# A hybrid decoder layer: plain products for the second pair of column tiles, one weight split fewer in every pair, and a reordered startup

## The chip, the cores and the metric

The kernel runs on one core of one Trainium2 chip. The metric is device time in microseconds (us), lower is better. Below, PE is the matrix engine (TensorE), DVE the vector engine, ACT the scalar engine, POOL is GpSimd and SP the engine that issues most transfers; PEld is the weight load of PE. A few tenths of a per cent separate repeated runs.

## What is computed

One layer is applied to a prompt of 1024 tokens and to 64 sample tokens (8 requests of 8 tokens). In short:

```
h      = RMSNorm(x, norm_pre)
proj   = h @ w_in                       # 1024 x 6656: seven slices of 512, three gates of 1024
a      = pool_mix(p_in) * silu(p_gate)
u      = c_val * sigmoid(c_glu)         # c_val: columns 1024.., c_glu: columns 1536..
bconv  = silu(LayerNorm(dwconv31(u))) * silu(c_gate)
cattn  = softmax(q @ mk) @ mv * silu(x_gate)      # mk, mv = RMSNorm(mem) @ w_mem_kv
merged = sum_n sigmoid(gate_n) * (branch_n @ w_branch[n])
y      = x + RMSNorm(merged @ w_out, norm_post)
```

The outputs are y for the prompt and the samples, the new memory keys and values, and the new states of the pooling and the convolution.

## The kernel before

**Numbers.** All is float32 in memory. For a product each operand is split by `hilo` (L74) into two float16 parts: ACT writes the high part (L75), DVE or POOL the rest (L77 without a factor, L79 with one). `mm3` (L81) then issues three matmuls for each block of 128 rows of the contraction (L85, L88, L89). An operand of 512 x 128 weights so costs one ACT and one DVE instruction for its split, and twelve matmuls for each 512 tokens.

**Pairs.** `w_in` is worked through in pairs of column tiles, 256 columns at a time, 26 pairs in all. The first pair (the first half of c_glu, columns from FIRST) is done with plain products inside `startup`. Each of the other 25 is a call of `pair` (L446), the first of them for c_val. With two tiles r, two halves kh of the contraction and two halves of the tokens a plain pair has eight products of 12 matmuls. `pair` uses seven: sums of the four weight blocks a11, a12, a21, a22 meet sums of the four input blocks. The input blocks and their sums are split once, into the seven sections B11, B21, B22, T1, T2, T3, T4 of the tile BO; the first half of the tokens as columns of h gives B11 and B21, the second gives B22 and (in two tiles b12) the block that `startup` alone uses; T1 to T4 are differences of both halves.

A pair is seven stages. `base0` (L494) splits a21 and a22, negates the second row of raw weights on ACT (L498) and adds them with an accumulating transfer issued by POOL (L499), which gives s1 = -(a21 + a22). `base1` (L502) splits a11 and a12 and issues three more accumulating transfers (L505 to L507) for s3, s2 and s4. The preps split the sums. `m0` to `m6` are the products and `e0` to `e6` take the results out of the matrix engine's memory: L513 is a copy on ACT, L466 (`post`) a scaled addition on DVE. `m5` also does the sample tokens with a11, a12, a22 and a21 against BS, the split sample columns.

**Order.** The stage list is emitted by the loop at the end of `hybrid_layer_kernel` (LDPR = 12 stages ahead for the loads, 3 for the preps, BASE = 8 for the sums). After each stage some steps of the convolution (`conv_step`) and of the side jobs (`job_step`: `states`, `mem_kv`, attention heads, ...) follow, at the two rates that RATES gives for each section. All this is the order in which the program is written; a scheduler then places the instructions on the engines' queues, and each queue runs in its order. Buffers are few: 20 of tag Q, 13 split weight blocks (ws), 4 raw weight pairs (raw), 4 + 4 banks (pm, pb).

**Startup.** `startup` (L236) is a generator, run at the end of the function with pieces of the first call of `pair` between its yields. It loads eight tiles of x (xt[0] to xt[7]), takes their squares on ACT (`rstds`, L169), turns them by `flip` (L225; four transposes on PE for 128 columns), multiplies by the norm's factors (L264) and splits the first half of the tokens into B11 and B21. Between these splits the squares of xt[4] to xt[7] are taken; then come those of the sample tile xs and of the two memory tiles. The first product `first(0, 0)` follows, then the scaling of xt[4:6] on ACT and xt[6:8] on DVE (L221, L223), the second halves by `second_half(k)` for k = 0 to 3 (L290: two flips, L292 and L295 on DVE, and splits into b12, B22 and T1), the splits of T2, and T3 and T4 from subtractions on POOL (L312, L313). The program puts products between: `first(1, 0)`, and a11 x B11 and a12 x B21 of the c_val pair.

Of the kernel before, what the change touches and what calls it, by code (L numbers as in the profile page):

```python
# [38 lines left out]
RATES = [(1.1, 2.2), (1.2, 1.4), (0.9, 1), (1, 1.2), (1.3, 1.4), (0.6, 1.8), (0.8, 0.9), (1.3, 0.2), (0.8, 1)]  # L39
# [7 lines left out]
def hybrid_layer_kernel(ctx, tc, i, o):  # L47
# [121 lines left out]
    def rstds(xs):  # L169
        ss = tiny([P, len(xs)])[: xs[0].shape[0]]  # L170
        for t, x in enumerate(xs):
            nc.scalar.activation(junk[: x.shape[0]], x, AF.Square, accum_out=ss[:, t : t + 1])
        return rstd_of(ss, 1.0 / D)

    BO = cst.tile([P, 7, 2, 4, HALF], F16, name="BO")
    junk = BO[:, 6].rearrange("p a k n -> p (a k n)")[:, : 2 * D].bitcast(F32)
# [24 lines left out]
    xt += [load(i["x_prompt"][0, t * P : (t + 1) * P, :], P) for t in range(8, 8)]  # L201
    xs = load(i["x_sample"].rearrange("b s d -> (b s) d"), NS)
    mems = [load(i["mem_prompt"][0, t * P : (t + 1) * P, :], P) for t in range(2)]
# [11 lines left out]
    BS = cst.tile([P, 2, KT, NS], F16, name="BS")  # L215
    g_pre = cst.tile([P, KT], F32, name="g_pre")
# [14 lines left out]
    def bo(n, k):  # L231
        return BO[:, n, 0, k, :], BO[:, n, 1, k, :]
# [3 lines left out]
    def startup():  # L236
# [24 lines left out]
        for k in range(KT):  # L261
# [20 lines left out]
        first(0, 0, [lambda k: bo(B11, k), lambda k: bo(B21, k)])  # L282
        scale_x(xt[4:6], rs_[0], True)
        scale_x(xt[6:8], rs_[1], False)
        first_w(1)
        first_w(3)
        b12 = [Q([P, 2, 2, HALF], F16) for _ in range(2)]
        tq = [Q([P, 2, HALF]) for _ in range(4)]

        def second_half(k):  # L290
# [6 lines left out]
            hilo(tq[k][:, 0], *bo(T1, k), -1.0)  # L297

        second_half(0)
        yield  # L300
        first(1, 0, [lambda k: bo(B11, k), lambda k: bo(B21, k)])
        yield
        for k in range(1, 4):
            second_half(k)
            yield
        for k in range(4):
            hilo(tq[k][:, 1], *bo(T2, k), -1.0)
        for r in range(2):
            first(r, HALF, [lambda k: (b12[k // 2][:, 0, k % 2], b12[k // 2][:, 1, k % 2]), lambda k: bo(B22, k)])
            for k in (2 * r, 2 * r + 1):  # L310
                t3, t4 = half(), half()
                nc.gpsimd.tensor_tensor(t3, tq[k][:, 1], hx[k][:, 0], ALU.subtract)  # L312
                nc.gpsimd.tensor_tensor(t4, hx[k][:, 1], tq[k][:, 1], ALU.subtract)  # L313
                hilo(t3, *bo(T3, k))
                hilo(t4, *bo(T4, k), eng=nc.gpsimd)
            if r:
                break
            nc.vector.tensor_scalar(xs, xs, xs_r, None, ALU.mult)
# [7 lines left out]
            hilo(hs_, BS[:, 0].rearrange("p k n -> p (k n)"), BS[:, 1].rearrange("p k n -> p (k n)"))  # L326
# [9 lines left out]
    def mem_kv():  # L336
        memT = [Q([P, 2, KT // 2, NMEM], F16) for _ in range(2)]
# [103 lines left out]
    def mm_smp(out, w, kh, start, stop):  # L441
        mm3(out, [(w[:, 0, k, :], w[:, 1, k, :], BS[:, 0, 4 * kh + k, :], BS[:, 1, 4 * kh + k, :]) for k in range(4)], start, stop)

    early = {}

    def pair(c0, dest, block, smp, sc=1.0 / WS):  # L446


        v = {}
# [21 lines left out]
        def prep0():  # L471
            if not ahead:
                prep_a11()
# [11 lines left out]
        def prep5():  # L485
            spl("a22", lambda: A(1, 1))
            spl("a21", lambda: A(1, 0))
# [6 lines left out]
        def base0():  # L494
            spl("a21", lambda: A(1, 0))
# [54 lines left out]
        def m5():  # L550
            v["s"] = pm()
            mm_smp(v["s"][:, :NS], v["w", "a11"], 0, True, False)
            mm_smp(v["s"][:, :NS], v["w", "a12"], 1, False, True)
# [779 lines left out]
    for _ in start:  # L1333
        pass
# [68 lines left out]
```

## Time and profile before

| what | value |
|---|---|
| runs of the kernel before | 931.22, 933.86, 935.12 us, median 933.86 us |
| the profiled execution | 930.47 us, of it the span of the profile 928.5 us |
| PE busy | 856.7 us (92%), 5765 matmuls |
| DVE busy | 732.8 us (79%), 1141 instructions |
| ACT busy | 453.3 us (49%), 964 instructions |
| POOL busy | 362.7 us (39%), 384 instructions |
| mean granted PE clock | 0.972 |

Times in the views are us from the start of the span. A busy PE is not a PE at its peak: the span of a matmul overlaps that of the next, so that the distance of two starts is what one costs. The profile attributes an instruction to the line of a helper (L75, L79), and the tile names tell which call it is: ws are split weights, BO the split inputs, raw the loaded weights.

### The profile page before, as it was taken

To read this page: it belongs to the slowest core of one execution; us is meant where nothing else is said; L and a number is where in the kernel's file an instruction comes from. 1 tells how busy PE (TensorE), PEld (TensorE's weight loads), DVE (VectorE), ACT (ScalarE), POOL (GpSimd) and SP (SyncE) were. 2 spreads that over 40 slices of the span, in tenths; PEclk is the share of its full clock that TensorE was granted. 3 is DMA by queue.
4 is the path that set the end of the run, shared out by engine and by line. 5 is a ranking of instruction groups with operands and counts; after the bars stand their busy time and mean duration, and the time that the engine had idled before them with its cause. 6 is when DMAs were issued, how large, how long until landed. Compare 5 with 4: busy or idle time off the path is not lost. (4 is left out here: it accounts for less than half of the span.)

```text
span 928.5 us, 15208 instructions
## 1 busy us (share of the span) xinstructions
PE 856.7 (92%) x5765; PEld 459.7 (50%) x5765; DVE 732.8 (79%) x1141; ACT 453.3 (49%) x964; POOL 362.7 (39%) x384
## 2 busy tenths in 40 slices
PE   5869999899999879999988989999999999977996
PEld 4325445454555445455444445555555555544542
DVE  4798598999967699999998977548565544699886
ACT  8757536654653614323345444446344443545542
POOL 1463243344243260311244665526364212276500
PEclk8889999999999889999999999999999999989998
DMA  8625742224466223244443335545554657311232
GB/s 300 175 47 161 202 107 55 59 70 114 117 223 159 92 38 91 59 91 93 101 106 86 79 92 100 120 115 106 117 114 114 127 131 226 95 35 46 70 125 91
DMA packets 99237, 103.23 MB, mean 111 GB/s; under 512 B 5230, under 2 KB 71780, under 8 KB 99148
## 3 DMA queue, kind: packets, MB, share of 16 engines
q1 hardware_dynamic: 82748, 68.24, 23.4%
q0 software_dynamic: 16416, 34.02, 20.4%
q8 instruction: 45, 0.74, 0.3%
q14 instruction: 28, 0.23, 0.1%
HBM read 62.37 MB, written 6.33 MB: 74 GB/s over the span
## 5 line engine op out<-in xcount | busy, mean ns | idle before, releaser
L85 PE MATMUL pm<-BO,ws 128*128 128x512 f16 x836 | 318.7, 383 | 20.3 <-ACT h L513 8.7
L88 PE MATMUL pm<-BO,ws 128*128 128x512 f16 x836 | 318.9, 381 | 2.2 <-DVE BO L79 1.6
L89 PE MATMUL pm<-BO,ws 128*128 128x512 f16 x836 | 318.3, 382 | 2.1 <-DVE ws L79 1.2
L79 DVE SCALAR_TENSOR_TENSOR ws<-raw,ws 128x512 f16<-128x512 f32 x228 | 194.3, 868 | 60.1 <-ACT ws L75 58.4
L88 PEld LDWEIGHTS <-ws 128*128 128x128 f16 x1548 | 148.9, 99 | 141.6 <-issue 35.6
L89 PEld LDWEIGHTS <-ws 128*128 128x128 f16 x1548 | 149.1, 99 | 124.5 <-issue 7.8
L85 PEld LDWEIGHTS <-ws 128*128 128x128 f16 x1548 | 148.5, 99 | 115.5 <-issue 6.4
L75 ACT ACTIVATE ws<-raw 128x512 f16<-128x512 f32 x228 | 138.4, 627 | 123.9 <-PE pm L89 55.9
L714 DVE SCALAR_TENSOR_TENSOR q<-q,cw,q 128x1024 f32<-128x1024 f32 x120 | 170.9, 1433 | 0.3
L85 PE MATMUL pb<-q,ws 128*128 128x364 f16 (+1 forms) x288 | 93.1, 326 | 5.7 <-DVE q L1151 5.7
L88 PE MATMUL pb<-q,ws 128*128 128x364 f16 (+1 forms) x288 | 93.8, 326 | 0.0
L89 PE MATMUL pb<-q,ws 128*128 128x364 f16 (+1 forms) x288 | 93.7, 325 | 0.0
L499 POOL DMA_DIRECT2D raw<-raw x25 | 22.0, 878 | 154.0 <-ACT raw L498 126.3
L513 ACT ACTIVATE h<-pm 128x512 f32<-128x512 f32 x75 | 44.2, 591 | 54.5 <-PE pm L89 49.9
L1151 DVE SCALAR_TENSOR_TENSOR q<-pb,q 128x364 f32<-128x364 f32 (+1 forms) x72 | 37.5, 529 | 24.9 <-PE pb L89 23.6
L466 DVE SCALAR_TENSOR_TENSOR q<-pm,h 128x512 f32<-128x512 f32 x51 | 34.9, 685 | 22.1 <-PE pm L89 13.2
L498 ACT ACTIVATE raw<-raw 128x512 f32<-128x512 f32 x50 | 31.1, 628 | 38.6 <-DVE ws L79 37.6
L75 ACT ACTIVATE q<-q 128x1024 f16<-128x1024 f32 (+2 forms) x37 | 35.6, 971 | 27.1 <-DVE q L863 16.9
L77 POOL TENSOR_TENSOR q<-q,q 128x1024 f16<-128x1024 f32 (+1 forms) x17 | 32.0, 1883 | 39.9 <-ACT q L75 39.9
L506 POOL DMA_DIRECT2D raw<-raw x25 | 21.8, 871 | 64.8 <-DVE ws L79 25.0
L85 PE MATMUL pm<-BS,ws 128*128 128x64 f16 x416 | 42.8, 193 | 4.0 <-DVE q L466 4.0
L507 POOL DMA_DIRECT2D raw<-raw x25 | 21.9, 877 | 61.0 <-issue 14.7
(242 smaller groups left out, 1305.8 us busy)
## 6 DMA issues: line engine op xcount, KB each, us to landing
raw<-in_w_in SPq DMA_DIRECT2D x104, 256.0 KB, 2.9
raw<-raw POOLq DMA_DIRECT2D x100, 256.0 KB, 3.2
q<-in_x_prompt SPq DMA_DIRECT2D x16, 512.0 KB, 9.0
q<-q POOLq DMA_DIRECT2D x14, 544.0 KB, 5.6
raw<-in_w_branch SPq DMA_DIRECT2D x24, 256.0 KB, 3.7
q<-in_w_mem_kv SPq DMA_DIRECT2D x8, 512.0 KB, 6.2
q<-in_cache_mem_k SPq DMA_DIRECT2D x8, 512.0 KB, 3.5
q<-in_cache_mem_v SPq DMA_DIRECT2D x8, 512.0 KB, 7.0
```

What stands on the lines that cost most here:

```text
L75: nc.scalar.activation(hi, src, AF.Copy, scale=scale)
L77: (eng or nc.vector).tensor_tensor(lo, src, hi, ALU.subtract)
L79: nc.vector.scalar_tensor_tensor(lo, src, scale, hi, ALU.mult, ALU.subtract)
L85: ins = nc.tensor.matmul(out, wh, xh, start=start and j == 0, stop=False, skip_group_check=partial)
L88: nc.tensor.matmul(out, wh, xl, start=False, stop=False, skip_group_check=partial)
L89: nc.tensor.matmul(out, wl, xh, start=False, stop=stop and j == n - 1, skip_group_check=partial)
L466: nc.vector.scalar_tensor_tensor(dst, ps, sc, base, ALU.mult, ALU.add)
L498: nc.scalar.activation(A(1, kh), A(1, kh), AF.Copy, scale=-1.0)
L499: nc.gpsimd.dma_start(out=A(1, 1), in_=A(1, 0), accum_op=ALU.add)
L513: nc.scalar.activation(v[name], ps, AF.Copy, scale=sc)
L714: ins = nc.vector.scalar_tensor_tensor(acc, src, wj, acc, ALU.mult, ALU.add)
L1151: nc.vector.scalar_tensor_tensor(g, p, 1.0 / WS, g, ALU.mult, ALU.mult)
```

## The change

Five things change.

- The first call of `pair` (c_val, columns from 1024) becomes `plain_pair`: eight products of the four split weight blocks with the operands that `startup` holds, no sums of weights, and three stages in place of seven. Two products (first half of the tokens) are issued inside `startup`, two and the samples are the three stages. The second pair's weights are loaded as before; those of the third pair (stages[3]) are now loaded inside `startup`, and the loads of `states` are issued there too.
- In every other pair a21 is no longer split. The samples use s1 with a negated first half of the sample columns (BSN) and a22 with the difference of both halves (BSD).
- The squares of xt[4] to xt[7] and of xs stand behind the splits of the first half and of all first weights; the scaling of xt[4:6] goes from ACT to POOL. The memory tiles are loaded, and their squares taken, in the job `mem_kv`, three steps later than before, with a Q tile as the squares' unused output.
- `second_half` is called for k = 0, 1, then k = 2, 3, with the products of the first half between. It no longer splits into T1. T1 is split behind `first(0, HALF)`; T2, T3 and T4 behind both products of the second half.
- `startup` is no generator any more, and the first rate of jobs is 4.8 a stage in place of 2.2, since that section has 3 stages in place of 7.

The core of the diff:

```diff
-RATES = [(1.1, 2.2), (1.2, 1.4), (0.9, 1), (1, 1.2), (1.3, 1.4), (0.6, 1.8), (0.8, 0.9), (1.3, 0.2), (0.8, 1)]
+RATES = [(1.1, 4.8), (1.2, 1.4), (0.9, 1), (1, 1.2), (1.3, 1.4), (0.6, 1.8), (0.8, 0.9), (1.3, 0.2), (0.8, 1)]
...
-    mems = [load(i["mem_prompt"][0, t * P : (t + 1) * P, :], P) for t in range(2)]
...
+    BSN = cst.tile([P, 2, KT // 2, NS], F16, name="BSN")
+    BSD = cst.tile([P, 2, KT // 2, NS], F16, name="BSD")
...
-            if k in (3, 7):
-                rs_.append(rstds(xt[k + 1 - k // 4 * 2 : k + 3 - k // 4 * 2]))
-
-        xs_r = rstds([xs])
-        mem["r"] = rstds(mems)
...
-        first(0, 0, [lambda k: bo(B11, k), lambda k: bo(B21, k)])
-        scale_x(xt[4:6], rs_[0], True)
-        scale_x(xt[6:8], rs_[1], False)
+        first(0, 0, early["ops", 0])
         first_w(1)
         first_w(3)
+        rs_ = [rstds(xt[4:6]), rstds(xt[6:8])]
+        xs_r = rstds([xs])
+        for t, x in enumerate(xt[4:6]):
+            nc.gpsimd.tensor_tensor(x, x, rs_[0][:, t : t + 1].to_broadcast([P, D]), ALU.mult)
+        scale_x(xt[6:8], rs_[1], False)
...
             hilo(p, *bo(B22, k), gk)
-            hilo(tq[k][:, 0], *bo(T1, k), -1.0)
+
+        first(1, 0, early["ops", 0])
+        early["split"](0)
         second_half(0)
...
+        second_half(1)
+        early["first"](0)
+        early["split"](1)
+        second_half(2)
+        second_half(3)
+        early["first"](1)
+        for f in stages[3][0]:
+            f()
+        stages[3][0] = []
+        job = states()
+        next(job)
+        jobs.append(job)
+        jobs.append(mem_kv())
         for r in range(2):
-            first(r, HALF, [lambda k: (b12[k // 2][:, 0, k % 2], b12[k // 2][:, 1, k % 2]), lambda k: bo(B22, k)])
...
+            first(r, HALF, early["ops", HALF])
             if r:
                 break
+            for k in range(4):
+                hilo(tq[k][:, 0], *bo(T1, k), -1.0)
...
+            n = KT // 2 * NS
+            hilo(hs_[:, :n], flat(BSN[:, 0]), flat(BSN[:, 1]), -1.0)
+            hd = half()[:, :n]
+            nc.vector.tensor_tensor(hd, hs_[:, n:], hs_[:, :n], ALU.subtract)
+            hilo(hd, flat(BSD[:, 0]), flat(BSD[:, 1]))
+        for k in range(4):
+            hilo(tq[k][:, 1], *bo(T2, k), -1.0)
+        for k in range(4):
+            t3, t4 = half(), half()
+            nc.gpsimd.tensor_tensor(t3, tq[k][:, 1], hx[k][:, 0], ALU.subtract)
+            nc.gpsimd.tensor_tensor(t4, hx[k][:, 1], tq[k][:, 1], ALU.subtract)
+            hilo(t3, *bo(T3, k))
+            hilo(t4, *bo(T4, k), eng=nc.gpsimd)
...
     def mem_kv():
+        mems = [load(i["mem_prompt"][0, t * P : (t + 1) * P, :], P) for t in range(2)]
+        yield
+        yield
+        yield
+        mem["r"] = rstds(mems, Q([P, D]))
...
+    def plain_pair(c0, block, smp):
+
+        raw, w = {}, {}
...
+        def split(r):
+            for kh in range(2):
+                w[r, kh] = new_ws()
+                hilo(raw[kh][:, r], w[r, kh][:, 0], w[r, kh][:, 1], WS)
+
+        def prod(r, t0):
+            p = pm()
+            for kh in range(2):
+                x = w[r, kh], early["ops", t0][kh]
+                mm3(p, [(x[0][:, 0, k, :], x[0][:, 1, k, :], *x[1](k)) for k in range(4)], kh == 0, kh == 1)
+            block(r, t0, p, 1.0 / WS)
...
+        early.update(load=[ldw(0), ldw(1)], split=split, first=lambda r: prod(r, 0))
+        for f in (lambda: prod(0, HALF), lambda: prod(1, HALF), samples):
+            stages.append([[], None, f, None, [], *rate, None])
+
     def pair(c0, dest, block, smp, sc=1.0 / WS):
+        if not stages:
+            plain_pair(c0, block, smp)
+            return
...
         def prep5():
             spl("a22", lambda: A(1, 1))
-            spl("a21", lambda: A(1, 0))
...
         def base0():
-            spl("a21", lambda: A(1, 0))
             spl("a22", lambda: A(1, 1))
...
-            mm_smp(v["s"][:, NS : 2 * NS], v["w", "a22"], 1, True, False)
-            mm_smp(v["s"][:, NS : 2 * NS], v["w", "a21"], 0, False, True)
+            mm_smp(v["s"][:, NS : 2 * NS], v["w", "a22"], BSD, True, False)
+            mm_smp(v["s"][:, NS : 2 * NS], v["w", "s1"], BSN, False, True)
```

More of the change, by code (lines that the diff above doesn't have):

```diff
@@ L439, in mm_op, with mm_smp, ldw, f @@
         mm3(out, [(w[:, 0, k, :], w[:, 1, k, :], BO[:, n, 0, k, :], BO[:, n, 1, k, :]) for k in range(4)], start, stop, True, pinned)
-    def mm_smp(out, w, kh, start, stop):
-        mm3(out, [(w[:, 0, k, :], w[:, 1, k, :], BS[:, 0, 4 * kh + k, :], BS[:, 1, 4 * kh + k, :]) for k in range(4)], start, stop)
+    def mm_smp(out, w, x, start, stop):
+        mm3(out, [(w[:, 0, k, :], w[:, 1, k, :], x[:, 0, k, :], x[:, 1, k, :]) for k in range(4)], start, stop)
+    BS0, BS1 = BS[:, :, : KT // 2], BS[:, :, KT // 2 :]
     early = {}
+    def plain_pair(c0, block, smp):
+        raw, w = {}, {}
+        def ldw(kh):
+            def f():
+                raw[kh] = load_pair(kh, c0)
+            return f
+        def split(r):
[8 more added lines that the diff above has]
+            block(r, t0, p, 1.0 / WS)
+        def samples():
+            p = pm()
+            for r in range(2):
+                for kh, x in enumerate((BS0, BS1)):
+                    mm_smp(p[:, r * NS : (r + 1) * NS], w[r, kh], x, kh == 0, kh == 1)
+            for r in range(2):
+                smp(r, p[:, r * NS : (r + 1) * NS])
+        early.update(load=[ldw(0), ldw(1)], split=split, first=lambda r: prod(r, 0))
+        for f in (lambda: prod(0, HALF), lambda: prod(1, HALF), samples):
+            stages.append([[], None, f, None, [], *rate, None])
     def pair(c0, dest, block, smp, sc=1.0 / WS):
+        if not stages:
+            plain_pair(c0, block, smp)
+            return
         v = {}
@@ L471, in prep0 @@
         def prep0():
-            if not ahead:
-                prep_a11()
+            prep_a11()
         def prep1():
@@ L569, in e6 @@
             block(0, HALF, c, None)
-        ahead = not stages
         preps = [prep0, prep1, prep2, prep3, prep4, prep5, prep6]
@@ L575, in pair @@
         loads = [ldw(0), ldw(1)]
-        if ahead:
-            early.update(
-                load=[*loads], first=lambda: (prep_a11(), m0(), e0()),
-                second=lambda: (prep3(), m3()))
-            loads, preps[3], mms[0], evs[0], mms[3] = [], None, None, None, None
         for j in range(7):
@@ L1323, in hybrid_layer_kernel @@
         stages[at + s][4].append(load_x(*tts))
-    start = startup()
     for f in early["load"]:
         f()
-    next(start)
-    next(start)
-    early["first"]()
-    next(start)
-    early["second"]()
-    for _ in start:
-        pass
+    startup()
     pps = pb()
```

31 lines of the change are left out of this document (9 added, 22 removed).

## The prediction

> **What bounds the kernel now.** I read the page's table of busy tenths first, then the busy times by stretch, then the groups and the timeline of the worst stretch.
>
> ```profile
> PE   5869999899999879999988989999999999977996
> DVE  4798598999967699999998977548565544699886
> ```
>
> A column is a fortieth of the span. PE is nearly always busy; it is thin in the first three columns and in single ones later, and DVE stands at 9 in the first half. The stretches put numbers to it (columns: length, then PE, PEld, DVE, ACT, POOL busy, granted clock, DMA share, GB/s):
>
> ```profile
> 19.00:70.00 51.00, 38.68 (x159) 17.03 (x159) 45.68 (x69) 35.87 (x63) 26.95 (x22) 0.83 0.46 118
> 70.00:96.00 26.00, 25.77 (x218) 14.89 (x217) 21.79 (x37) 19.51 (x39) 8.49 (x11) 1.00 0.61 172
> 96.00:110.00 14.00, 14.00 (x71) 6.88 (x70) 4.20 (x8) 4.98 (x9) 2.84 (x3) 1.00 0.73 210
> 110.00:300.00 190.00, 180.68 (x1284) 99.72 (x1283) 168.87 (x253) 103.64 (x226) 73.38 (x69) 1.00 0.44 115
> 300.00:500.00 200.00, 183.20 (x1299) 98.99 (x1298) 188.31 (x218) 80.52 (x153) 63.44 (x51) 0.97 0.35 81
> 500.00:560.00 60.00, 55.76 (x345) 27.43 (x344) 48.52 (x57) 27.97 (x51) 38.06 (x32) 0.97 0.39 95
> 560.00:810.00 250.00, 249.65 (x1693) 136.64 (x1692) 148.86 (x239) 115.33 (x227) 101.80 (x98) 1.00 0.56 127
> ```
>
> From 560 to 810 PE never waits: there only matmuls count. From 110 to 560 PE idles 9.3 + 16.8 + 4.2 = 30 us, beside a DVE that is busy 89% and 94% in the two long stretches. The startup, 19 to 70, has the most to give: 12 us without any matmul, at a mean clock of 0.83. How much PE time it really wastes, the PE groups of that stretch tell:
>
> ```profile
> L85 PE MATMUL pm<-BO,ws 128*128 128x512 f16 x35 | 14.7, 419 | 2.0 <-ACT BO L75 2.0
> L89 PE MATMUL pm<-BO,ws 128*128 128x512 f16 x32 | 13.1, 410 | 1.2 <-DVE ws L79 1.2
> L88 PE MATMUL pm<-BO,ws 128*128 128x512 f16 x32 | 12.8, 401 | 2.2 <-DVE BO L79 1.6 <-DVE BO L77 0.6
> L228 PE MATMUL pb<-ident,q 128*128 128x128 f32 x26 | 5.5, 336 | 3.8 <-DVE BO L79 2.5 <-DVE q L264 0.7 <-DVE q L79 0.3
> L88 PE MATMUL pm<-q,ws 128*128 128x512 f16 x8 | 4.0, 497 | 0.0
> L89 PE MATMUL pm<-q,ws 128*128 128x512 f16 x8 | 3.8, 474 | 0.0
> L85 PE MATMUL pm<-q,ws 128*128 128x512 f16 x8 | 3.4, 493 | 3.6 <-ACT q L75 3.6
> ```
>
> That is 35 + 32 + 32 + 8 + 8 + 8 = 123 large matmuls. What one costs is the distance of two starts:
>
> ```profile
> 19.01 0.58 PE L85 MATMUL pm<-BO,ws 128*128 128x512 f16 x1 [0.70 <-ACT BO L75]
> 25.35 0.57 PE L85 MATMUL pm<-BO,ws 128*128 128x512 f16 x1
> 37.21 0.38 PE L85 MATMUL pm<-BO,ws 128*128 128x512 f16 x1
> 39.59 0.38 PE L89 MATMUL pm<-BO,ws 128*128 128x512 f16 x1
> 42.84 0.59 PE L85 MATMUL pm<-q,ws 128*128 128x512 f16 x1 [2.87 <-ACT q L75]
> 45.02 0.63 PE L89 MATMUL pm<-q,ws 128*128 128x512 f16 x1
> 45.45 0.63 PE L85 MATMUL pm<-q,ws 128*128 128x512 f16 x1
> ```
>
> Eleven steps from 37.21 to 39.59 are 0.216 us each; after the pause the step is 0.43, twice that. So 123 x 0.216 + 5.5 for the transposes (their busy time, an upper bound) = 32 us of work lie in 51 us: 19 us are lost. About 4 of them are the ramp from 19.01 to 25.35, in which ten steps go by (2.2 us) among waits and a slow clock. From there to 39.59 nothing is lost. The other 15 come after 39.59: the products of the first half have run out, and the operands of the second half come one by one. Why they come late, DVE and POOL show:
>
> ```profile
> 31.22 1.42 DVE L223 TENSOR_SCALAR q<-q,t 128x1024 f32<-128x1024 f32 x2
> 36.65 1.90 DVE L79 SCALAR_TENSOR_TENSOR ws<-raw,ws 128x512 f16<-128x512 f32 x3 [2.18 <-ACT ws L75]
> 44.16 3.00 DVE L152 TENSOR_SCALAR t<-t 128x2 f32<-128x2 f32 x1
> ```
> ```profile
> 44.31 1.59 POOL L312 TENSOR_TENSOR h<-q,q 128x512 f32<-128x512 f32 x1
> 45.54 1.58 POOL L313 TENSOR_TENSOR h<-q,q 128x512 f32<-128x512 f32 x1
> ```
>
> The rows are scaled by 32.6, but DVE first waits for the weight sums s1, s2, s3 of the c_val pair (split at 36.65, behind ACT and transfers); then a tiny instruction of the memory tiles' root takes 3.00 us while POOL does two subtractions for T3 and T4. Between the second halves stand the splits for T1 and T2, which no early product needs.
>
> **The change, part by part.**
>
> *Plain products.* Seven products of twelve matmuls become eight: +12 x 0.216 = +2.6 us on PE, which is busy anyhow. The sample products keep their number. In return the first half of the tokens feeds 4 x 24 = 96 matmuls, where before it fed 24 + 24 + 12 + 12 = 72: 5.2 us more of stock. The second half feeds another 96 before any of T1 to T4 is wanted. Four splits, two negations and four accumulating transfers of the c_val pair go, and with them the wait of 2.18 us at 36.65. What is late next is the flips of the second half.
>
> *Readiness of the second half.* In the new program ACT first splits, then takes squares:
>
> ```profile
> 24.24 0.62 ACT L75 ACTIVATE ws<-raw 128x512 f16<-128x512 f32 x1
> ```
> ```profile
> L172 ACT ACTIVATE BO<-q 128x1024 f32<-128x1024 f32 x10 | 10.5, 1051 | 3.6 <-DMA q<-in_x_prompt 3.4
> L986 POOL TENSOR_TENSOR q<-q 128x1024 f32<-128x1024 f32 x1 | 2.3, 2346 | 0.1
> ```
> ```profile
> L292 DVE SCALAR_TENSOR_TENSOR q<-pb,g_pre,q 128x512 f32<-128x512 f32 x4 | 3.0, 739 | 0.0
> L79 DVE SCALAR_TENSOR_TENSOR BO<-q,BO 128x512 f16<-128x512 f32 x8 | 9.9, 1232 | 0.0
> ```
>
> Before, that run of splits ended near 24.9. Without a square and two scalings ahead of it (estimate 3 us, three instructions of the size of L172) it ends near 22. Four squares of 1.05 us and their small reads end at 27; the root and its small DVE steps take 2 to 4; then POOL scales two tiles, a shape that the trace does not show on POOL in this form: 2 x 2.35 by L986, at least 2 x 1.42 / 2 by DVE's L223, and I take POOL's. The rows are ready at 34 to 36, some 2 to 3 us later than the 32.6 of before. Then 16 DVE instructions of 0.74 us (four for each k) and two evictions follow, 13 us, to about 48 or 49, with k = 0, 1 ready near 42. PE has first-half work until 39.6 + 5.2 = 45, and the products of k = 0, 1, half of the 96, can bridge 10 us more if the queue has them in that order. Where it takes all four k of one operand first, PE waits 3 to 4 us. I take 2.
>
> *T1 to T4 later.* They cost the same and are wanted by the third pair. That starts near 72 (49, and 96 x 0.216 = 20.7, and samples); its second product wants T1 at 75, its sixth T4 at 72 + 5 x 12 x 0.216 = 85. DVE has from 49 to 75 the splits of T1, T2, T3 (12 x 0.7 = 8), seven of the third pair (5) and evictions and samples (6): 19 us in 26. That cover is thin, since POOL runs 8 subtractions and 4 splits of 1.6 us at the same time, and L79 into BO took 1.23 us on average beside them. I take 2 us of PE wait for it, bounds 0 and 9 (rival C). BSN, BSD and the difference add three DVE instructions, each no longer than a weight split (0.87), on work off the path.
>
> *Memory tiles.* Their loads leave the SP queue ahead of the c_val weights:
>
> ```profile
> 14.27 1.04 SPq L166 DMA_DIRECT2D q<-in_mem_prompt  x2
> 20.17 2.70 SPq L195 DMA_DIRECT2D raw<-in_w_in  x4
> ```
>
> So those weights come 1 to 2 us sooner, in time for the second pair of products; the memory loads then wait for Q tiles of x (free near 46) and stand behind the loads of `states` and of the third pair. Everything they feed is three job steps later; the first section still runs 14 steps (15 before), and the heads that want the keys start only at the end of the third pair, by when the remaining eight steps have run. I cost this at nothing on the path; if the keys' products fall in a gap it is below nothing, by up to 2 us, and the same above if they miss it.
>
> *One split fewer in 24 pairs.*
>
> ```profile
> L79 DVE SCALAR_TENSOR_TENSOR ws<-raw,ws 128x512 f16<-128x512 f32 x228 | 194.3, 868 | 60.1 <-ACT ws L75 58.4
> L75 ACT ACTIVATE ws<-raw 128x512 f16<-128x512 f32 x228 | 138.4, 627 | 123.9 <-PE pm L89 55.9
> ```
> ```profile
> L79 DVE SCALAR_TENSOR_TENSOR ws<-raw,ws 128x512 f16<-128x512 f32 x126 | 109.5, 881 | 11.5 <-ACT ws L75 11.5
> ```
>
> 24 x 0.87 = 21 us of DVE and 24 x 0.63 = 15 us of ACT go. It pays only where PE waits for DVE, from 110 to 560: the last row counts 126 splits there, about 14 pairs, so 12 us of DVE. PE lost 30 us there, not all to DVE. Bounds 0 and 12; I take a third, 4 us. After 560 it is hidden behind PE.
>
> **The sum.** Lost in the startup after: ramp 4 + order of k 2 + T's 2 = 8, against 19: -11. Plain products +2.6. Splits -4. Together -12.4 us. The profiled execution took 930.5, so 918.1; from the median of the runs, 933.9, it is 921.5. I forecast between them, **920**.
>
> Does the lead survive? DVE must keep up. Before, it idled after the startup:
>
> ```profile
> 105.02 0.69 DVE L79 SCALAR_TENSOR_TENSOR ws<-raw,ws 128x512 f16<-128x512 f32 x1 [7.77 <-ACT ws L75]
> ```
>
> From 70 to 110 DVE was busy 26 of 40 us. A lead of 8 to 9 us has to come out of those 14 idle ones, so it fits; from 110 on DVE is the tight engine and the rates tie its work to the stages.
>
> **A rule of the skill against it.** The row at 44.16 showed a small DVE instruction held for 3.00 us through two POOL subtractions. The Trainium skill, page "SBUF — State Buffer", section "Who interferes with whom", says that GpSimd and DVE share one pair of ports as an exclusive lock, taken by a DVE instruction with two SBUF inputs against a GpSimd instruction that reads SBUF; the trace agrees in the size of the hold (3.00 against 1.59 + 1.58 us). By that rule the scaling on POOL would hold DVE's first-half splits too, up to 4.7 us, and the sum would be nearer -8.
>
> **Rivals.**
>
> *A. The DVE backlog eats the lead.* T's, sums and memory splits fall into one stretch and PE waits there for what it gained: T's cost 9 instead of 2, splits bring 1: -2.4 in all, 928 to 931. For it: DVE was busy 45.7 of the 51 us from 19 to 70 already. Against: 14 idle us behind it. The same time results if the scheduler, which places by its own timeline, does not put the pieces where the program has them.
>
> *B. DVE pays fully.* From 110 to 560 every split saved is PE time (12 instead of 4) and the ramp falls by 2: -22, 908 to 912. For it: DVE at 94% from 300 to 500. Against: many of PE's waits there are chains, not load.
>
> *C. Slower, by POOL.* POOL has eight subtractions and four splits of 1.6 us for the T's, and in its queue, in order, the accumulating transfers of the third pair, each behind the one before:
>
> ```profile
> POOL raw L505 <- DMA raw<-raw: 46.1, 19, 3.5
> ```
>
> If POOL and DVE exclude each other wholly, the subtractions for k = 0, 1 hold the second halves of k = 2, 3 by 4 x 1.6 = 6.4 us, and T4 is ready at 49 + 8 + 19 + 11 (T splits, POOL, DVE's other work) = 87, 2 after it is wanted: the 9 us of the upper bound, and the sum is still -5. If three waits of 3.5 us in POOL's queue also stand ahead of the subtractions, T4 comes some 10 us later still, and the sum is +5: 936 to 939. It decides when PE has waited over 14 us for the T's, that is, with T4 beyond 99.
>
> **Chances and range.** Forecast (914 to 927) 0.62, A 0.18, B 0.12, C 0.08. What a measurement of this kernel can tell from no change is about 0.5%, so 929.2 to 938.5 counts as the same. Faster: the forecast, B and about half of A, 0.82; same: the rest of A and a third of C, 0.12; slower 0.06. The range takes in the forecast, most of A and half of B: 909 to 931.
>
> **What would show it.** PE from 19 to the end of the c_val pair without a pause of 2 us; 24 matmuls of each product with ws and q behind the flips; DVE with no L79 into BO for T1 between L292 and L295 of one group; second halves done by 50; the samples of c_val taken out near 72; 200 weight splits instead of 228; PE's idle time from 110 to 560 down from 30 to about 26. It would be wrong if the flips start after 38, if PE stands before T1 to T4, or if the first tap of the convolution is no earlier than before.

## The result, and the profile after

| | runs | median | range |
|---|---|---|---|
| before | 4 | 932.54 us | 930.89 to 935.12 |
| changed | 4 | 946.40 us | 944.99 to 947.06 |

The ratio is 1.0159 with the interval 1.0122 to 1.0197: the change makes the kernel slower by 1.6%, where 920 us was forecast. The profiled execution of the changed kernel has a span of 943.2 us, 14.7 more than before.

The page of the changed kernel, busy time and the busy tenths of PE and DVE:

```profile
PE 859.8 (91%) x5777; PEld 461.0 (49%) x5777; DVE 733.5 (78%) x1116; ACT 431.3 (46%) x931; POOL 360.7 (38%) x379
PE   5896998999999879999989899999999999977996
DVE  5797588999978899999978977638635543689886
```

The count says that the change does what it should: 12 matmuls more on PE, and DVE and ACT with fewer instructions. In PE's tenths the third column has become better (9 for 6) and the fourth worse: 6 for 9, a hole that was not there before. The stretches of the changed kernel (columns as in the prediction):

```profile
19.00:70.00 51.00, 44.35 (x219) 20.78 (x220) 43.03 (x70) 31.48 (x57) 18.61 (x17) 0.91 0.55 142
70.00:96.00 26.00, 16.99 (x147) 10.28 (x145) 19.76 (x26) 11.67 (x27) 13.45 (x13) 0.87 0.21 47
110.00:300.00 190.00, 180.09 (x1283) 100.22 (x1281) 169.07 (x246) 101.28 (x223) 77.03 (x66) 0.99 0.45 116
300.00:500.00 200.00, 183.37 (x1279) 99.03 (x1278) 182.48 (x204) 74.13 (x142) 61.81 (x51) 0.96 0.37 88
500.00:560.00 60.00, 52.97 (x351) 25.99 (x347) 52.10 (x52) 23.99 (x46) 34.17 (x28) 0.94 0.33 76
```

From 19 to 70 the startup gains what was meant: 219 matmuls in place of 159, at a clock of 0.91 in place of 0.83. From 70 to 96 PE is busy 17.0 us, before 25.8. From 500 to 560 it is busy another 2.8 us less, at a lower clock.

To see where a lead comes and goes, I added up the columns of all matmul records in order of time, and read off when the same amount of work is done in each kernel. The table gives that moment against the one before (negative: ahead), at five times of the kernel before. The changed kernels have 12 matmuls (2.6 us) more, so that an end at +12.1 is a span 14.7 us longer. Near a wait a number jumps by the length of the wait. A float32 transpose counts as its 128 columns here although it takes about twice as long as they would (eight in 0.90 us in e16, from 84.77 to 85.67); counted double, the leads at 80 are some 1.5 us smaller, and from 100 on nothing changes. The names are those of the runs in the next section.

| kernel | ratio to before | at 80 | 100 | 460 | 500 | 580 | end |
|---|---|---|---|---|---|---|---|
| the changed kernel | 1.0159 | -9.0 | +3.6 | +2.3 | +4.9 | +10.4 | +12.1 |
| e4, es on DVE | 1.0158 | -7.9 | +1.2 | +1.1 | +0.2 | +7.3 | +12.3 |
| e5, taps back in step | 1.0091 | -8.9 | +4.7 | +2.6 | +4.5 | +2.9 | +4.0 |
| e14, e5 and a later negation | 1.0092 | -9.0 | +3.6 | +2.4 | +5.5 | +6.1 | +7.0 |
| e13, split of a21 back | 1.0024 | -10.1 | -5.1 | -4.0 | -7.1 | -1.2 | +1.2 |
| e17, split back in four pairs | 1.0121 | -10.0 | -5.2 | -3.1 | +0.4 | +6.6 | +12.2 |
| e11, e5 and split back | 1.0015 | -10.6 | -5.8 | -4.2 | -5.3 | -3.0 | -2.5 |
| e16, e5 and split back in four pairs | 0.9976 | -10.4 | -5.5 | -6.8 | -3.5 | -2.8 | -2.5 |

The changed kernel is 9.0 us ahead at 80, loses 12.6 by 100 and another 5.5 between 500 and 580. Of the 4 us that it loses from 460 to 480, e1 below shows the place.

**The first place.** The timeline of PE in the changed kernel (start, duration, engine, line, what; in brackets the idle time and its releaser), then that of ACT, SP and POOL:

```profile
84.47 0.63 PE L376 MATMUL pb<-ident,q 128*128 128x128 f32 x4
92.36 1.12 PE L376 MATMUL pb<-ident,q 128*128 128x128 f32 x4 [7.26 <-ACT es L445]
93.27 0.63 PE L85 MATMUL pm<-BO,ws 128*128 128x512 f16 x1
93.69 0.63 PE L88 MATMUL pm<-BO,ws 128*128 128x512 f16 x1
```
```profile
80.12 1.14 ACT L439 ACTIVATE us<-pb 128x240 f32<-128x240 f32 x4
91.20 0.63 ACT L555 ACTIVATE raw<-raw 128x512 f32<-128x512 f32 x1 [9.94 <-DMA raw<-in_w_in]
91.74 0.57 ACT L445 ACTIVATE es<-pb 128x480 f32<-128x480 f32 x1
```
```profile
85.99 8.67 SPq L196 DMA_DIRECT2D raw<-in_w_in  x3
```
```profile
80.44 0.86 POOL L563 DMA_DIRECT2D raw<-raw  x1
81.05 2.56 POOL L77 TENSOR_TENSOR BO<-h,BO 128x512 f16<-128x512 f32 x2
85.89 0.87 POOL L564 DMA_DIRECT2D raw<-raw  x1 [2.28 <-DVE ws L79]
```

The queue of SP (who waited for whom from 70 to 100: us in total, times, longest) and DVE show what the load stood for:

```profile
SPq L196 <- DVE ws L79: 31.0, 1, 31.0
```
```profile
79.41 4.76 DVE L77 TENSOR_TENSOR BO<-h,BO 128x512 f16<-128x512 f32 x2
84.69 1.28 DVE L79 SCALAR_TENSOR_TENSOR ws<-raw,ws 128x512 f16<-128x512 f32 x2
```

Read it from PE backwards. Transposes of the memory tiles stand in PE's queue before the third pair's first product. They want a bank (pb) that ACT has yet to empty into es, a copy of 0.57 us for the job `states`. In ACT's queue, one place ahead of it, is the negation (L555) of the fifth pair's raw weights, which wait for their load. The load is issued at 85.99, since the four raw tiles hold the third and the fourth pair until their sums are made and split: SP had waited for a weight split of DVE, which ended at 85.97. That split stood behind two splits of T3 on DVE, 4.76 us long beside POOL's two for T4 (81.05). So 0.57 us of work off the path holds PE for 7.26 us, and the next matmuls come 0.43 us apart in place of 0.216.

**The second place.** DVE, POOL and PE of the changed kernel:

```profile
524.72 5.78 DVE L765 SCALAR_TENSOR_TENSOR q<-q,cw,q 128x1024 f32<-128x1024 f32 x2
530.42 1.48 DVE L526 SCALAR_TENSOR_TENSOR h<-pm,h 128x512 f32<-128x512 f32 x2
```
```profile
521.43 7.99 POOL L1037 TENSOR_TENSOR q<-q 128x1038 f32<-128x1038 f32 x3 [11.77 <-DVE q L526]
```
```profile
531.15 0.58 PE L85 MATMUL pm<-BO,ws 128*128 128x512 f16 x1 [3.58 <-DVE h L526]
```

Two taps of the convolution (L765, 1.28 us alone) take 5.78 while POOL adds up the pooling windows. The eviction L526, which PE needs, stands behind them in DVE's queue, and PE waits 3.58 us; its clock from 530 to 540 is then 0.67.

### The profile page after: what moved, and what is told of

Same layout as the page of the kernel before. It is cut to its first block, busy times and chain, and to the rows that moved or that the text cites. A ratio compares the mean times of both kernels' runs of the same rounds, so it can differ in the third digit from the quotient of the medians.

```text
span 943.2 us, 15131 instructions
## 1 busy us (share of the span) xinstructions
PE 859.8 (91%) x5777; PEld 461.0 (49%) x5777; DVE 733.5 (78%) x1116; ACT 431.3 (46%) x931; POOL 360.7 (38%) x379
## 5 line engine op out<-in xcount | busy, mean ns | idle before, releaser
L79 DVE SCALAR_TENSOR_TENSOR ws<-raw,ws 128x512 f16<-128x512 f32 x200 | 166.6, 850 | 42.5 <-ACT ws L75 41.6
L765 DVE SCALAR_TENSOR_TENSOR q<-q,cw,q 128x1024 f32<-128x1024 f32 x120 | 170.5, 1426 | 0.6
L75 ACT ACTIVATE ws<-raw 128x512 f16<-128x512 f32 x200 | 119.7, 624 | 97.5 <-PE pb L89 33.4
L555 ACT ACTIVATE raw<-raw 128x512 f32<-128x512 f32 x48 | 30.0, 628 | 96.4 <-DMA raw<-in_w_in 57.3
L570 ACT ACTIVATE h<-pm 128x512 f32<-128x512 f32 x72 | 42.3, 589 | 68.3 <-PE pm L89 62.6
L556 POOL DMA_DIRECT2D raw<-raw x24 | 22.3, 931 | 129.5 <-ACT raw L555 127.6
L526 DVE SCALAR_TENSOR_TENSOR q<-pm,h 128x512 f32<-128x512 f32 x48 | 32.7, 683 | 27.3 <-PE pm L89 16.2
L563 POOL DMA_DIRECT2D raw<-raw x24 | 20.7, 862 | 78.8 <-DVE ws L79 32.0
L564 POOL DMA_DIRECT2D raw<-raw x24 | 20.7, 864 | 75.8 <-DVE ws L79 25.0
L77 POOL TENSOR_TENSOR q<-q,q 128x1024 f16<-128x1024 f32 (+1 forms) x17 | 36.1, 2126 | 31.8 <-ACT q L75 29.8
L715 ACT ACTIVATE q<-q 128x512 f32<-128x512 f32 x36 | 22.6, 628 | 52.3 <-DVE q L526 52.2
```

Of the source, the lines that this page charges most:

```text
L75: nc.scalar.activation(hi, src, AF.Copy, scale=scale)
L77: (eng or nc.vector).tensor_tensor(lo, src, hi, ALU.subtract)
L79: nc.vector.scalar_tensor_tensor(lo, src, scale, hi, ALU.mult, ALU.subtract)
L526: nc.vector.scalar_tensor_tensor(dst, ps, sc, base, ALU.mult, ALU.add)
L555: nc.scalar.activation(A(1, kh), A(1, kh), AF.Copy, scale=-1.0)
L570: nc.scalar.activation(v[name], ps, AF.Copy, scale=sc)
```

## The experiments

Each line of numbers is the median, the ratio to the kernel before measured beside it, and its interval.

**e1.** The kernel before, with only the split of a21 left out (samples by BSN and BSD as in the change).

```diff
-            spl("a21", lambda: A(1, 0))
             spl("a22", lambda: A(1, 1))
```


> The kernel before with one part of the change alone: a21 is not split, the samples use s1 and a22 with the negated half and the difference. Startup, order and rates are those of before. Theory M (the startup gives its lead back through one queue, and the split saved is a gain of its own): 2 to 5 us faster than before, 928 to 931 where before takes 932.5, with 25 weight splits fewer (203 of 128x512 into ws). Rival R (what costs time after 470 us comes from the split saved or from the longer use of s1): 5 to 8 us slower than before, 938 to 941, lost between 460 and 550 us. Rival N (DVE time saved is hidden and only the order of the queues moves): within 3 us either way.

932.96 us, 0.9998 (0.9975 to 1.0020). 25 splits fewer are worth nothing by themselves. The kernel is 2 to 7 us ahead between 150 and 460, and 2.7 behind at 480. PE and ACT of e1 at that place:

```profile
470.88 0.59 PE L85 MATMUL pm<-BO,ws 128*128 128x512 f16 x1 [5.33 <-ACT h L521]
```
```profile
468.77 1.06 ACT L75 ACTIVATE q<-q 128x1024 f16<-128x1024 f32 x1 [6.51 <-DVE q L1000]
470.26 0.57 ACT L521 ACTIVATE h<-pm 128x512 f32<-128x512 f32 x1
```

The kernel before has the two the other way round (PE waits 3.37 us for its copy, L513, 2.0 less than in e1):

```profile
470.40 0.57 ACT L513 ACTIVATE h<-pm 128x512 f32<-128x512 f32 x1
471.92 1.04 ACT L75 ACTIVATE q<-q 128x1024 f16<-128x1024 f32 x1
```

So without the split ACT's queue has another order here too: a split of q that waits for DVE stands ahead of the copy that PE needs. In this order are also the changed kernel (PE waits 3.12 us for the copy), e2, e3, e4, e5, e9, e14, e16 and e17; the wait is 0.25 us in e4 and 3.1 to 5.3 in the others. The five kernels of full convolution that split a21 in every pair (before, e6, e11, e13, e15) have the copy first, and so have e10, e12 and e18.

**e2.** The changed kernel with the old rate of jobs.

```diff
-RATES = [(1.1, 4.8),
+RATES = [(1.1, 2.2),
```


> The changed kernel with the first rate of jobs back at 2.2 a stage (6 steps in the first section in place of 14), so that the transposes of the memory tiles and of the states no longer stand ahead of the third pair on the matrix engine. Theory M: the wait of 7.3 us for the state's eviction near 85 us goes, 7 to 9 us faster than the changed kernel (937 to 940), unless the delayed memory keys hold the attention heads. Rival D (DVE is the tight engine, and the lead would be lost to T3, T4 and the weight sums anyway): the first result of the third pair is taken out at 115 us as before the edit, and the time stays within 2 us of 946.4.

949.08 us, 1.0189 (1.0148 to 1.0230). Without the steps the pause at 85 is gone (-0.9 at 100), the loss between 500 and 580 is there (+7.2 to +10.0), and more is lost behind it (+17.7 at the end). That the side jobs are too many at the start is not the cause.

**e3.** The third and fourth pair's base sums written ahead of T3 and T4.

```diff
+        for s in (3, 4):
+            stages[s][7]()
+            stages[s][7] = None
         for k in range(4):
             t3, t4 = half(), half()
```


> The changed kernel, with the sums of the third pair's weights put ahead of the subtractions for T3 and T4 in the program, so that POOL's accumulating transfers and the splits go first and the raw tiles come free earlier. Theory M: the load of weights that was issued at 86.0 us goes out 10 us or more earlier, the negation on ACT no longer holds the state's eviction, and the kernel is 6 to 9 us faster than the changed one (937 to 940). Rival D: T3 and T4 come later instead, the matrix engine waits for them, and the time stays within 2 us of 946.4 or grows.

946.94 us, 1.0164 (1.0127 to 1.0202); PE waits 7.4 us for es as before. The edit removes neither the pause nor any time.

**e4.** es is taken out by DVE.

```diff
-        nc.scalar.activation(es[...], p[...], AF.Copy)
+        nc.vector.tensor_copy(es[...], p[...])
```


> The changed kernel, with the one eviction of the pooling state copied out by DVE in place of ACT, so that it no longer stands behind the negation of weights on ACT. Theory M: the matrix engine's wait of 7.3 us near 85 us shrinks below 2 us and the third pair starts 6 to 8 us earlier; 5 to 8 us faster than the changed kernel (938 to 941) if nothing downstream takes it back. Rival D: the wait moves to the next product that needs DVE, and the time stays within 2 us of 946.4.

945.76 us, 1.0158 (1.0119 to 1.0197). The pause falls from 7.3 to 2.1 us, so ACT's queue is its cause; but the kernel, 0.2 behind at 500, is 7.3 behind at 580. A second loss takes the place of the first.

**e5.** The rate of taps. Before, the first section had 7 stages with 1.1 taps each and left a fraction of 0.7; 3 stages leave 0.3, and from then on some stages emit their taps one stage later. 3 x 0.9 leaves 0.7 again.

```diff
-RATES = [(1.1, 4.8),
+RATES = [(0.9, 4.8),
```


> The changed kernel, with the first convolution rate at 0.9 in place of 1.1. No tap exists in that section, so only the fraction that is carried into the next one changes: 3 x 0.9 leaves 0.7, as the kernel before does (7 x 1.1 = 7.7), where the change leaves 0.3. From the third pair on the taps fall on the same stages as before the change. Theory P (the stretch from 460 to 560 us is lost because the taps moved by a stage against the pooling, an order the rates were chosen for): 6 to 9 us faster than the changed kernel, 937 to 940. Rival D (DVE and POOL set the pace from 110 to 560 and absorb any lead): within 3 us of 946.

939.90 us, 1.0091 (1.0062 to 1.0120). The first pause stays (7.5 us), the second loss is gone: +4.5 at 500, +2.9 at 580. The profiled execution is the fastest of the seven, 3.0 us under their median, so that the end of its row in the table is about as much too low.

**e6.** The kernel before with 7 x 1.043 = 7.3, the fraction of the change.

```diff
-RATES = [(1.1, 2.2),
+RATES = [(1.043, 2.2),
```


> The kernel before, with the first convolution rate at 1.043, so that 7 stages leave a fraction of 0.3 as in the changed kernel. Nothing else is touched, and no work is added or left out. Theory P: 5 to 9 us slower than before (938 to 942), lost between 460 and 560 us. Rival D: within 3 us of before.

936.45 us, 1.0060 (1.0035 to 1.0085), with 4.6 us lost between 500 and 580. A change that does no other work and moves a tap by a stage costs 0.6%.

**e7 and e8.** The kernel before and the changed one with every second tap on 64 columns. The convolution is incomplete in both; DVE has some 60 x 1.2 us less to do.

```diff
-            acc, src = Y[ch][:, :S], U[ch][:, j : j + S]
+            m = NS if j % 2 else S
+            acc, src = Y[ch][:, :m], U[ch][:, j : j + m]
```


> The kernel before, with every second tap of the convolution done on 64 columns in place of 1024 (60 of 124 taps, so the convolution is left incomplete). That takes some 60 x 1.2 = 72 us from DVE between 110 and 560 us and leaves every instruction in place. Rival D: DVE no longer sets the pace there, PE's 30 us of waits shrink by 10 to 20. Theory P: the waits come from the order of the queues, and less than 5 us go.

> The changed kernel with the same lightened taps (every second one on 64 columns, the convolution left incomplete). Rival D: with DVE relieved the lead of 9 us at 80 us survives at least in part, so this is no slower than the lightened kernel before, or up to 9 us faster. Theory P: it stays 8 to 14 us slower than the lightened kernel before, as the full ones do.

925.36 us, 0.9938 (0.9904 to 0.9973), and 922.48 us, 0.9903 (0.9867 to 0.9939). With DVE relieved the changed kernel is not slower any more, though its pause at 85 is still 7.7 us. At 100 it is 4.3 behind the kernel before and e7 is 2.0 behind; at 460 they are 12.0 and 8.1 ahead. So a lead or a loss made before 110 does not by itself decide the end: with a light DVE it is made up by 460.

**e9, e10, e12.** e5 with es on DVE; with a fifth raw tile; with the old rate of jobs.

```diff
-        return sb.tile([P, 2, 4, P], F32, tag="raw", bufs=4, name=nm("raw"))
+        return sb.tile([P, 2, 4, P], F32, tag="raw", bufs=5, name=nm("raw"))
```


> The changed kernel with both edits: the fraction of the taps restored (first rate 0.9) and the pooling state's eviction on DVE. If the stall near 85 us and the moved taps are two separate losses, they add: 2 to 3 us less than with the taps alone, 935 to 938 where that takes 939. If the lead is absorbed by DVE after 110 us all the same, 938 to 941.

> The changed kernel with the fraction of the taps restored and five raw weight tiles in place of four, so that a half of the fifth pair's weights need not wait for the third pair's sums. If the late weights are what holds ACT's negation, and through it the state's eviction and the matrix engine, the wait of 7.5 us near 85 us shrinks below 3 us and the kernel takes 932 to 937; if not, the wait stays and the time is 938 to 941.

> The changed kernel with the first rates at 0.9 and 2.2: the taps' fraction restored, and 6 job steps in the first section in place of 14. With 2.2 alone the lead of 8 us lived to 90 us and was lost later. If only the moved taps lost it: 930 to 936. If the order after 200 us loses it for another reason: 940 to 944.

937.50 us, 1.0057 (1.0025 to 1.0089); 936.98 us, 1.0060 (1.0033 to 1.0087); 940.98 us, 1.0099 (1.0071 to 1.0127). With the fifth tile the pause at 85 is gone and the kernel is 3.8 ahead at 100: the negation waits for its load, and the load for a tile. Neither cure beats the kernel before.

**e11.** e5 with the split of a21 restored in all pairs.

```diff
         def base0():
+            spl("a21", lambda: A(1, 0))
             spl("a22", lambda: A(1, 1))
```


> The changed kernel with the fraction of the taps restored and a21 split again in the 24 pairs (samples by a21 and a22 as before the change). 21 us more of DVE and 15 of ACT. If the split saved is worth time where DVE is the tight engine: 3 to 6 us slower than without it (942 to 945). If it is hidden, as alone on the kernel before: within 3 us of 939.

933.49 us, 1.0015 (0.9993 to 1.0038). 24 splits more, 21 us of DVE by the page's mean (its busy total rises by 13.5, from 728.8 in e5 to 742.3), make it 6.4 us faster; neither case of the expectation has that. Between 70 and 110 PE now waits 2.0 us at the longest.

**e13.** The split restored, with the rate of taps left at 1.1.

> The changed kernel with the split of a21 restored in every pair (samples by a11, a12, a21, a22 as before), the rate of taps left at 1.1. Theory: the early negation and the shifted taps are two separate losses that add up. Then this run gains over the changed kernel what the split gained with the taps in place, 939.9 - 933.5 = 6.4 us: 939 to 941, no pause of PE over 4 us between 80 and 95, and the loss of some 6 us between 460 and 540 still there. Rival: the split only helps because of where it puts the work beside the taps; then 944 to 947.

932.70 us, 1.0024 (1.0005 to 1.0043), where 939 to 941 was expected by adding up. So of the five parts of the change, taking back the missing split alone undoes nearly all of the loss: 946.4 against 932.7. Taking back the taps' fraction alone undoes 6.5 us (e5). The two losses do not add up: e13 still loses 5.9 us between 500 and 580, but it comes there 7.1 ahead.

The groups show how a split that goes can cost. ACT's negation before, after, and in e13 (busy, mean; then the idle time ahead of it and its releaser):

```profile
L498 ACT ACTIVATE raw<-raw 128x512 f32<-128x512 f32 x50 | 31.1, 628 | 38.6 <-DVE ws L79 37.6
```
```profile
L555 ACT ACTIVATE raw<-raw 128x512 f32<-128x512 f32 x48 | 30.0, 628 | 96.4 <-DMA raw<-in_w_in 57.3
```
```profile
L557 ACT ACTIVATE raw<-raw 128x512 f32<-128x512 f32 x48 | 29.9, 627 | 44.6 <-DVE ws L79 44.1
```

The negation overwrites a21. With the split it may run only when DVE has read a21; without it, it needs the load alone, so the scheduler places it earlier, and ACT stands 96 us ahead of negations in place of 39 or 45, mostly for loads. Most of these waits cost nothing: they are 98 us in e1, which is no slower than the kernel before, and 77 in e16 below. What counts is who stands behind one of them.

**e14.** e5 with the negation and its transfer moved from `base0` to `base1`, behind the splits of a11 and a12.

> The changed kernel with the rate of taps 0.9 and no split of a21, but the negation of the raw second row and its accumulating transfer are written one stage later, behind the splits of a11 and a12. Theory: what costs is the early place of the negation in ACT's queue, where it waits for the weights' load. Then the pause of PE at 84 to 93 goes and the time is near that of the run with the split restored: 933 to 937. Rival 1: the place in the program is not what sets it, and the raw tile comes free too late in any order: the pause stays and it takes 939 to 941. Rival 2: the sums s1 to s4 come a stage later and their four transfers in a row are now late for the preps: new waits of PE for ws, over 941.

939.02 us, 1.0092 (1.0064 to 1.0120): rival 1. The pause stays (7.45 us), and in ACT's queue the negation still stands between us and es. Here the place in the program is not what orders the queue; what the instruction depends on (the split, in e11 and e16) is.

**e16 and e17.** a21 split in the four pairs behind the plain one only, with the rate of taps 0.9 and 1.1.

```diff
+        both = len(stages) < 3 + 7 * 4
...
-            spl("a22", lambda: A(1, 1))
+            if both:
+                spl("a21", lambda: A(1, 0))
+            spl("a22", lambda: A(1, 1))
```


> The changed kernel with the rate of taps 0.9 and a21 split in the four pairs behind the plain one only; the other 20 pairs go without it. Theory: the missing split costs only at 84 to 93, where a negation waits in ACT's queue; then nearly all of the 6.4 us comes back and 20 splits of DVE remain saved: 931 to 935. Rival: the early negations cost a little in every pair up to 560, where PE waits for DVE and ACT: then the gain is about a third of 6.4 us, 937 to 939.

> The changed kernel with a21 split in the four pairs behind the plain one only, and nothing else altered (rate of taps 1.1). Theory: the one early negation in ACT's queue is nearly the whole loss, and the shifted taps cost 1 to 2 us when PE comes without that pause: 930 to 934, no pause over 4 us between 80 and 95. Rival: the shifted taps cost 5.6 us on their own, as they did on the kernel before: 935 to 938.

e16: 929.82 us, 0.9976 (0.9956 to 0.9997). Four pairs give back at least as much as all 24 do: with the taps in step, what the missing split costs comes back with the first pairs. ACT in e16:

```profile
81.62 1.14 ACT L439 ACTIVATE us<-pb 128x240 f32<-128x240 f32 x4
82.69 0.60 ACT L445 ACTIVATE es<-pb 128x480 f32<-128x480 f32 x1
...
94.31 0.63 ACT L559 ACTIVATE raw<-raw 128x512 f32<-128x512 f32 x1 [0.76 <-DVE ws L79]
```

es comes out right behind us, and the negation 12 us later, behind DVE. From 70 to 96 PE of e16 is busy 22.7 us at full clock:

```profile
70.00:96.00 26.00, 22.73 (x181) 12.87 (x180) 23.54 (x33) 17.09 (x36) 13.56 (x14) 1.00 0.43 113
```

e17: 944.76 us, 1.0121 (1.0068 to 1.0175); both of its theories fail. The first pause is gone, and yet it ends where the changed kernel does. Up to 460 it stays within 3 us of e13. Then it loses 3.5 us by 500, where e13 gains 3.1: ACT's queue near 470 is in the order of e1, and PE waits 3.12 us. It loses 6.2 us between 500 and 580, e13 5.9, and 5.6 more behind them, e13 2.4. So with the fraction 0.3 the missing split costs some 12 us in the later 20 pairs (944.8 against 932.7), and what e16 says of the first pairs holds for taps in step alone. DVE and PE of e17:

```profile
521.41 5.78 DVE L769 SCALAR_TENSOR_TENSOR q<-q,cw,q 128x1024 f32<-128x1024 f32 x2
```
```profile
527.84 0.38 PE L85 MATMUL pm<-BO,ws 128*128 128x512 f16 x1 [3.58 <-DVE h L526]
```

These are the rows of the second place again. Over all runs with the full convolution the second place goes with the fraction of the taps alone: the seven kernels with 0.3 (the changed one, e2, e3, e4, e6, e13, e17) lose 2.8 to 7.1 us between 500 and 580, the ten others -1.6 to +2.3, and in those seven alone PE waits there for an eviction into h by DVE (0.7 to 3.6 us).

**e15 and e18.** A fifth raw tile on e11 and on e16.

> The changed kernel with the rate of taps 0.9, a21's split restored, and five raw tiles instead of four. Theory: with the split back no queue waits for the raw tiles, so a fifth brings nothing: 932 to 935, the same as the kernel before. Rival: loads that start earlier keep the lead of the startup through the stretch that DVE bounds; then as much is gained as the fifth tile brought without the split, 939.9 - 937.0 = 3 us: 930 to 931.

> The changed kernel with the rate of taps 0.9, a21 split in four pairs only, and five raw tiles. Theory: no queue waits for raw tiles any more, so it stays within 2 us of the run with four raw tiles, 928 to 932. Rival: in the 20 pairs without the split the early negations still wait for loads, and the fifth tile lets them come sooner: 926 or less.

930.70 us, 1.0002 (0.9978 to 1.0025), and 930.87 us, 1.0004 (0.9977 to 1.0031). The kernels with four raw tiles have 1.0015 and 0.9976, so a fifth tile shows no gain that can be told once the first pause is gone (e15's median lies in the range of its rival, but the intervals of e15 and e11 overlap). The best version is e16, 0.24% faster than the kernel before, at the edge of what can be told.

## Why the prediction was wrong

**Right: what the startup gains.** Forecast were 11 us; the changed kernel is 9.0 ahead at 80, and 10.0 to 10.6 in e11, e13, e16 and e17 (some 1.5 less with the transposes counted double). PE idles 6.7 us between 19 and 70, before 12.3. The second half came later, though. DVE and ACT of the changed kernel:

```profile
35.53 1.40 DVE L224 TENSOR_SCALAR q<-q,t 128x1024 f32<-128x1024 f32 x2
42.83 1.29 DVE L79 SCALAR_TENSOR_TENSOR ws<-raw,ws 128x512 f16<-128x512 f32 x2 [3.96 <-ACT ws L75]
47.51 0.68 DVE L79 SCALAR_TENSOR_TENSOR BO<-q,BO 128x512 f16<-128x512 f32 x1
61.60 0.74 DVE L79 SCALAR_TENSOR_TENSOR BO<-pb,g_pre,BO 128x512 f16<-128x512 f32 x1
```
```profile
42.17 1.15 ACT L75 ACTIVATE ws<-raw 128x512 f16<-128x512 f32 x2 [5.26 <-DMA raw<-raw]
```

The last tiles were scaled by 36.9 (forecast 34 to 36), but the last split of a second half (61.60, into B22) ends at 62.3, not at 48 or 49. DVE waited 3.96 us for ACT, which stood 5.26 us behind a weight sum of a later pair. And all eight splits of T1 and T2, of which 47.51 is the first, stand in DVE's queue among the second halves, though the program has them behind: the prediction named a T1 split there as a sign of being wrong. PE's longest wait between 34 and 70 is 2.3 us all the same.

**Within its bound: DVE held by the scaling on POOL.** The prediction priced it by the Trainium skill, page "SBUF — State Buffer", section "Who interferes with whom", at up to 4.7 us, and the trace agrees. POOL and DVE of the changed kernel:

```profile
22.77 4.57 POOL L287 TENSOR_TENSOR q<-q,t 128x1024 f32<-128x1024 f32 x2
27.31 1.60 POOL L77 TENSOR_TENSOR BO<-q,BO 128x512 f16<-128x512 f32 x1
```
```profile
22.62 2.98 DVE L79 SCALAR_TENSOR_TENSOR ws<-raw,ws 128x512 f16<-128x512 f32 x2
25.52 2.38 DVE L77 TENSOR_TENSOR BO<-q,BO 128x512 f16<-128x512 f32 x1
27.82 1.64 DVE L79 SCALAR_TENSOR_TENSOR ws<-raw,ws 128x512 f16<-128x512 f32 x1
```

Four splits of 0.68 us each (2.7) took 7.0, so 4.3 us of hold. The first was not held; the next two took 2.38 each beside the scalings, 3.4 us of hold, and the last 1.64 beside a split of POOL's (27.31), another 1.0. POOL's two scalings took 4.57 (forecast 2 x 2.35). The 9.0 us at 80 are what is left with that paid. The row at 44.16, which the prediction took as a first agreement, is a TENSOR_SCALAR with one tensor as its input, so the sentence on two SBUF inputs does not speak of it; the held splits have two.

**Right: the plain products**, 12 matmuls.

**Wrong, the step that failed: "One split fewer in 24 pairs", -4 us with bounds 0 and 12.** It was sized as DVE time saved. Even that was less than the 21 us of the sum: DVE's busy total falls by 13.7 in e1 (719.1 against 732.8). Alone the missing split is worth 0 (e1), and in the new program it costs 6.4 us with the taps in step (medians of e5 and e11; 7.1 by the ratios) and 13.7 without (the changed kernel and e13; 12.6 by the ratios). PE's idle time from 110 to 560, forecast to fall from 30 to 26 us, is 9.9 + 16.6 + 7.0 = 33.5. The bound of 0 was the error of method: I took away a reader of a21 and did not ask what had waited for it. The row was on the page: `L498` waits 37.6 of its 38.6 us for `DVE ws L79`. What waited for the instruction taken out, ACT's negation, came free earlier and was placed in front of an urgent copy.

**Wrong: "Does the lead survive?"** I compared loads (14 idle us of DVE between 70 and 110). Most of the lead went in one wait, of ACT (PE 7.3 us, and then matmuls at half the pace), with DVE idle beside it: DVE is busy 19.8 of the 26 us from 70 to 96, before 21.8.

**Not seen: the rate of taps.** The prediction counted job steps of the first section, 14 and 15, and not that 3 stages of 1.1 leave another fraction than 7. e5 and e6 show it in both directions, 6.5 and 5.6 us by differences of medians or ratio.

**Memory tiles**, costed at nothing on the path: their transposes are the matmuls that stand in PE's queue at 84.47 and 92.36. Without the wait for es (e16) they cost nothing that shows.

**T1 to T4**, 2 us forecast: in e16 PE's longest wait between 70 and 110 is 2.0 us, and none of them is for BO. Rival C had the right sign and the wrong deciding point, T4 beyond 99. T4 was split by 83.6. That POOL and DVE hold each other, which C named, has its part in the chain all the same: T3's two splits of 4.76 us on DVE delay the weight split that lets a raw tile go at 85.97.

**Rivals A and B.** A lead is lost between 110 and 560, and with a light DVE it is not (e7 and e8), as A says, though in e1 what eats it is the order of ACT's queue; its 928 to 931 is near what the kernels without the pause and with a split reach (e11, e13, e16: 929.8 to 933.5). B, where every split saved is PE time, is refuted by e1.

What stays open: how the missing split changes the order of ACT's queue near 470 (e10, e12 and e18 lack it there too and keep the order), and what e17 (5.6 us) and the changed kernel (1.7) lose behind 580. e14 and e5, alike in time, differ by 3.2 us at 580; that is about what e5's profiled execution lies under its median.

## What to carry to other kernels

Before an instruction is taken out, look up who waits for it: its releases fix the order of other queues, and an instruction that becomes free early can stand in front of an urgent one and wait there for something slow (9.94 us here). Count waits at the head of an in-order queue, not only busy time. Where work is spread by rates, keep the phase of the spread when the number of stages changes, or measure it alone; here it costs 5.6 to 6.5 us, more than the best version gains (2.2).

## What the runs showed of the hardware

The first tap of each convolution tile on DVE (one tensor of 1024 columns, two single columns as factors) takes 0.81 us at its shortest. In the changed kernel one of the four took 11.16; POOL's group beside it follows:

```profile
327.94 11.16 DVE L763 TENSOR_SCALAR q<-q,cw,parT 128x1024 f32<-128x1024 f32 x1 [1.51 <-PE pb L89]
```
```profile
327.70 8.76 POOL L776 TENSOR_TENSOR q<-us,cw 128x992 f32<-128x992 f32 x4
336.12 2.41 POOL L77 TENSOR_TENSOR q<-q,q 128x1024 f16<-128x1024 f32 x1
```

DVE ends at 339.10, just behind POOL's last instruction (338.53): POOL ran five in a row, 10.8 us, and the tap lasted from the first to the last. In e17 the same tap took 10.97 us; in before, e5, e11, e13 and e16 it took 0.96 to 2.60. In the second place above each of the two taps ends 1.1 us behind one of POOL's sums (the second and the third). DVE's busy total does not show the splits saved: its weight splits fell from 194.3 us (the prediction's row) to 166.6, but the total rose from 732.8 to 733.5:

```profile
L79 DVE SCALAR_TENSOR_TENSOR ws<-raw,ws 128x512 f16<-128x512 f32 x200 | 166.6, 850 | 42.5 <-ACT ws L75 41.6
```

What all of DVE's instructions took above the shortest of their own kind adds up to 114 us before and 133 in the changed kernel, 18.5 more. It is 128 in both e5 and e11, which differ in the split alone, so this came with the rest of the change and is not what the saved splits turned into; how much of it is POOL's doing was not measured apart.
